# Gate and up products of the feed-forward stages as two by two blocks with seven half-size products

## The chip, the core and the metric

The kernel runs on one core of a Trainium2 chip. The metric is device time in microseconds (us) of one execution of the whole program. The engines that matter are TensorE (PE for its matmuls, PEld for its loads of stationary operands), VectorE (DVE), ScalarE (ACT), GpSimd (POOL) and SyncE (SP), whose queue issues nearly all DMAs.

## The reference, cut to what matters

Two layers of a token mixer and a SwiGLU feed-forward stage over 512 latent and 256 context tokens of width 1024, all float32. Layer 0 carries all 768 tokens; layer 1 computes its feed-forward stage on the 512 latent tokens alone. The change lies in the first product of this stage:

```python
FF_HIDDEN = 2816
def swiglu(h, w_i, w_o):
    g, u = jnp.split(h @ w_i, 2, axis=-1)      # (T,1024) @ (1024, 2*2816)
    return (jax.nn.silu(g) * u) @ w_o
...
xl = xl + ml[5] * rms_norm(swiglu(adaln(xl, g[2], ml[3], ml[4]), w_ffn_in[l], w_ffn_out[l]), g[3])
```

`ml` are per-layer modulation vectors, `silu(c) @ w_mod + b_mod`.

## The kernel before, in words

**Numbers.** A float32 product is made of three float32r matmuls (`mm3`): each operand x is kept as a rounded part hi and a rest lo = x - hi, and hi*hi + hi*lo + lo*hi are summed in PSUM. ACT writes hi, DVE writes lo (one subtraction with two inputs in SBUF). The weights come from DRAM in pieces of 128x1024 into three raw tiles on the chip (`NR = 3`), are split into one of five weight slots (`NW = 5`, `pump`), and the raw tile is then free for the next DMA. Pieces are loaded in one fixed order, `build_seq`. Weights are in reg7r, raw tiles and small things in reg8f; the residual stream X0 is reg6f; the two big regions at A0 (reg0, reg1) and B0 (reg2, reg3) swap roles between layers.

**Feed-forward stage (`ffn`).** The 22 units of 128 hidden columns are taken in groups of 4, 4, 4, 4, 2, 4. For each unit the gate piece and the up piece (128x1024 each: eight blocks of 128 along the inner dimension) are the stationary operands. In layer 0 the tokens stream in two parts of 512 and 256 columns, in layer 1 in one part of 512. So a unit is 2 pieces x 8 blocks x 3 = 48 matmuls for each part. After it, ACT takes the silu of the gate out of PSUM, DVE multiplies it with the up product out of PSUM, and hi and lo of the result are written. After each group the second weight matrix is applied: for each tile of 128 tokens and each half of 512 output columns 3 matmuls per unit of the group (the "w_o stretch" below), and DVE adds the sum to an accumulator in SBUF.

**Modulation vectors on DVE (`gemv_v`).** 56 raw pieces of `w_mod` (one modulation of layer 0, six of layer 1) are interleaved with the weights of layer 0's stage. Each is used by DVE as multiply-adds of 512 columns with two SBUF inputs (four for each of the first 24 pieces, two for each of the other 32); a piece holds one of the three raw tiles until then. PE transposes the results.

**Order.** All instructions are emitted by one program on the host. `Clock` keeps a modelled time for each engine and buffer; `drive` advances the main line (PE's products) and steps side lanes when their modelled due time has come. On the chip every engine runs its own list in order and waits on semaphores. In `Clock` the engines run side by side and never slow each other.

Of the kernel before, what the change touches and what calls it, by code (L numbers as in the profile page):

```python
# [13 lines left out]
ALU = mybir.AluOpType  # L14
# [136 lines left out]
class Builder:  # L151
    def __init__(self, tc, ctx, ins, out):
# [7 lines left out]
        cuts = [A0, A0 + 6144, B0, B0 + 6144, C0, VB, X0, W0, RAW0, self.L.end]  # L160
        self.reg = [[a, b, None, None] for a, b in zip(cuts, cuts[1:])]
        for i, k in enumerate('rrfffffrf'):
            self.mode(i, k)
        self.M = gp.tile([128, 7, 128], U8, name="M")
# [6 lines left out]
        self.narrow = False  # L171
# [20 lines left out]
    def V(self, off, *dims, p0=0, np_=128):  # L192
        a, b, t = self.find(off)
        t0 = t[:, off - a:off - a + 1]
        ps = t0.ap[0][0]
        return bass.AP(t0.tensor, t0.offset + p0 * ps, [[ps, np_]] + [list(d) for d in dims])
# [26 lines left out]
    def mm(self, out, lhsT, rhs, start=True, stop=True):  # L223
        n, m = self.cols(rhs), self.cols(lhsT)
        if rhs.dtype == F32R:
            t = max(0.417 * n, 105)
# [9 lines left out]
        self.nc.tensor.matmul(out, lhsT, rhs, start=start, stop=stop)  # L236

    def mm3(self, out, lh, ll, rh, rl, start, stop):
        r = self.r
        self.mm(out, r(lh), r(rh), start, False)  # L240
        self.mm(out, r(lh), r(rl), False, False)
        self.mm(out, r(ll), r(rh), False, stop)
# [119 lines left out]
    groups = [4, 4, 4, 4, 2, 4]  # L362

    def build_seq(self):
# [15 lines left out]
        for l in range(DEPTH):  # L380
# [23 lines left out]
            for gi, g in enumerate(self.groups):  # L404
                for i in range(2 * f, 2 * (f + g)):
                    w(I['wfi'][l, i])
                    if l == 0 and i > 3 and spread:
                        raw(spread.pop(0), 'g')
                for i in range(f, f + g):
                    w(I['wfo'][l, i])  # L410
                if l == 0:
# [3 lines left out]
        self.seq, ns = [], 0  # L415
        for a, k in seq:
            self.seq.append([a, k, ns, None])
            ns += k == 'w'
# [5 lines left out]

    def pump(self, upto=-1):
        seq, go = self.seq, True
        while go:
            go = False
            if self.n_dma < len(seq) and self.slots:
                it = seq[self.n_dma]  # L430
                it[3] = RAW0 + self.slots.pop(0) * 1024
                self.dma(self.S(it[3], 1024), it[0])
                self.n_dma += 1
                go = True
            while self.n_proc < self.n_dma and seq[self.n_proc][1] != 'w':
                self.n_proc += 1
            if (self.n_proc < self.n_dma and seq[self.n_proc][2] < self.n_freed + NW
                    and (self.n_proc <= upto or self.ck.written(self.S(seq[self.n_proc][3], 1024)) <= self.now + 200)):
                it = seq[self.n_proc]
                w = W0 + (it[2] % NW) * 2048  # L440
                rw = self.S(it[3], 1024)
                if self.n_proc >= self.n_hi:
                    self.act(self.r(self.S(w, 1024)), rw)
                if self.sides[2] and self.nbk == 2 and self.ck.t['po'] + 1200 < self.ck.t['dv']:

                    self.pool(self.r(self.S(w + 1024, 1024)), rw, self.S(w, 1024), ALU.subtract, 2360)
                else:
                    self.tt(self.r(self.S(w + 1024, 1024)), rw, self.S(w, 1024), ALU.subtract)
                self.slots.append((it[3] - RAW0) // 1024)
                self.n_proc += 1  # L450
                go = True

    def get(self):

        while self.seq[self.n_w][1] != 'w':
            self.n_w += 1
        k = self.n_w
        self.n_w += 1
        while k >= self.n_proc:
            self.pump(k)  # L460
            if k >= self.n_proc:
                self.more(force=True)
        assert k < self.n_proc, "stuck"
        return W0 + (self.seq[k][2] % NW) * 2048
# [6 lines left out]
    def get_raw(self, tag='g'):  # L471
# [5 lines left out]
        return self.seq[k][3]  # L477
# [5 lines left out]
    def extra_time(self):  # L483
# [7 lines left out]
        return max(self.ck.written(self.S(self.seq[k][3], 1024)), busy) if k < self.n_dma else None  # L491
# [199 lines left out]
    def proj_t(self, H, tiles, npc, n, cb, ok=None):  # L691
        ws = []
        per = 8 // npc
        for i, t in enumerate(tiles):
            if ok:
                yield lambda: ok(t)
                yield self.ck.written(self.V(H + t * 128, (T, 16), (1, 128)))
# [220 lines left out]
    def attention(self):  # L918
# [100 lines left out]
        def restack():  # L1019
            for hh in range(2):  # L1020
                if hh not in restacked and issued > last[hh] and self.n_prep == 4:
# [3 lines left out]
                    if len(restacked) == 2:  # L1025
                        self.mode(5, 'f')
# [38 lines left out]
    def mixer(self):  # L1065
# [11 lines left out]
        self.mode(0 if l else 2, 'f')  # L1077
# [42 lines left out]
        self.mode(0 if RB == A0 else 2, 'r')  # L1120
        self.mode(5, 'r')
# [110 lines left out]
    def wout(self):  # L1232
# [79 lines left out]
    def wout_norm(self, t, junk):  # L1312
# [4 lines left out]
        self.scaled(t, y)  # L1317
        self.sides[1].append(self.wout_ada(t, y))
# [9 lines left out]
    def ffn(self):  # L1328
# [3 lines left out]
        TS, G5 = A + 6144, A + 9216  # L1332
# [3 lines left out]
        self.mode(1 if A == A0 else 3, 'f')  # L1336

        def unit(wg, wu, slot, parts, free=0):
            bs = {}
            for w in (wg, wu):  # L1340
                for o, n in parts:
                    b = self.bank()
                    bs[w, o] = self.B(b, n)
                    for kc in range(8):
                        self.mm3(bs[w, o], self.S(w + kc * 128, 128), self.S(w + 1024 + kc * 128, 128),
                                 self.S(H2 + kc * T + o, n), self.S(H2 + (8 + kc) * T + o, n), kc == 0, kc == 7)
                        if kc == 7 and w == wu:
                            k = slot % 2
                            s, fu = self.S(TS + k * 1536 + o, n), self.S(TS + k * 1536 + 768 + o, n)
# [347 lines left out]
```

## Time and profile before

| what | value |
|---|---|
| median of 3 runs | 1883.36 us (1878.64 to 1889.82) |
| profiled execution, its own time | 1883.15 us |
| its span in the trace | 1881.0 us, mean granted TensorE clock 0.991 |
| PE busy in the span | 1812.2 us (96%), 11140 matmuls |
| DVE busy | 1040.1 us (55%) |
| ACT busy | 684.0 us (36%) |
| POOL busy | 208.1 us (11%) |

Layer 0's feed-forward stage runs from about 500 to 1110 us after the start of the span, layer 1's from about 1500 us to the end. The 0.00 of the windows below is the start of the span. A row of a windows view has the window, its length, and busy time and number of instructions of PE, PEld, DVE, ACT and POOL, then the granted clock, the DMA share and GB/s. A row of a timeline has start, duration from first start to last end, engine, line, operation, operands and count. A matmul's duration is longer than the distance to the next one, because matmuls overlap; the distance between starts is what a stream of them costs. The same holds, to a smaller degree, for DVE.

### The profile page before, as it was taken

The numbers are of one execution on the slowest core, as the hardware profiler recorded it, in microseconds if no ns is written. First come the engines' busy times: TensorE is split into PE (matmuls) and PEld (weight loads), VectorE is DVE, ScalarE is ACT, GpSimd is POOL, SyncE is SP. The second block draws the span as 40 slices with busy tenths as digits, with TensorE's granted clock in tenths as the row PEclk, the third lists the DMA queues.
The fourth block names the chain that finished last, engine by engine and source line by source line (L and its number), as shares of the span: only waits on it lengthen the run. The fifth ranks groups of instructions, "written<-read, shape, count | busy, mean of one in ns | idle before, by whom it ended". The sixth has DMA issues, their size and how long they took to land.

```text
span 1881.0 us, 27410 instructions
## 1 busy us (share of the span) xinstructions
PE 1812.2 (96%) x11140; PEld 1507.5 (80%) x11140; DVE 1040.1 (55%) x1781; ACT 684.0 (36%) x1374; POOL 208.1 (11%) x287
## 2 busy tenths in 40 slices
PE   6999999997999999999999999999998989999998
PEld 3888886676789888888888878888776788888886
DVE  3478853566475666555455374887476542433444
ACT  4533431357473221212212264333266543222222
POOL 0000003234220000000000040000434100000002
PEclk9999999998999999999999999999999999999999
DMA  9211118442123433434343212111431223243221
GB/s 343 68 57 35 35 53 202 143 83 62 52 106 99 148 124 112 149 120 144 110 144 107 68 45 72 52 46 57 90 79 33 69 88 101 70 121 101 90 90 56
DMA packets 52782, 179.88 MB, mean 96 GB/s; under 512 B 6960, under 2 KB 7856, under 8 KB 52656
## 3 DMA queue, kind: packets, MB, share of 16 engines
q1 hardware_dynamic: 48816, 169.48, 28.3%
q0 software_dynamic: 3840, 8.65, 3.3%
q8 instruction: 87, 1.43, 0.3%
q14 instruction: 39, 0.32, 0.1%
HBM read 167.36 MB, written 2.10 MB: 90 GB/s over the span
## 4 chain that ended last, share of the span: by engine, by line
PE 85%; DVE 5%; ACT 5%; DMA 2%; issue 1%; POOL 1%; SPq 0%; DVEq 0%; POOLq 0%; ACTq 0%
PE P L236 82%; PE P L246 3%; ACT reg1f L257 1%; ACT reg3f L257 1%; DVE reg8f L959 1%; ACT reg7r L257 1%; DVE reg7r L264 1%; ACT reg8f L257 1%; DMA reg4f<-in_wmod 0%; DMA reg8f<-in_wmod 0%; DMA reg0r<-reg5r 0%; DVE reg4f L264 0%; DMA reg8f<-in_wout 0%; ACT reg0r L257 0%; DVE reg8f L276 0%
## 5 line engine op out<-in xcount | busy, mean ns | idle before, releaser
L236 PE MATMUL P<-reg2r,reg7r 128*128 128x256 f32 (+1 forms) x1920 | 481.0, 338 | 0.2 <-ACT reg8f L257 0.2
L236 PE MATMUL P<-reg0r,reg7r 128*128 128x512 f32 (+1 forms) x1344 | 380.3, 363 | 3.9 <-ACT reg0r L257 3.9
L264 DVE TENSOR_TENSOR reg7r<-reg8f,reg7r 128x1024 fp32r<-128x1024 f32 x200 | 243.1, 1225 | 232.7 <-ACT reg7r L257 231.1
L236 PEld LDWEIGHTS P<-reg2r,reg7r 128*128 128x128 f32 x1920 | 330.2, 190 | 39.1 <-issue 0.7
L257 ACT ACTIVATE reg7r<-reg8f 128x1024 fp32r<-128x1024 f32 x204 | 212.8, 1053 | 369.0 <-issue 150.8
L236 PE MATMUL P<-reg7r,reg0r 128*128 128x512 f32 (+1 forms) x1272 | 328.5, 389 | 8.1 <-ACT reg0r L257 6.1
L236 PE MATMUL P<-reg3r,reg7r 128*128 128x512 f32 (+1 forms) x960 | 321.9, 335 | 0.4 <-DVE reg3r L264 0.4
L236 PEld LDWEIGHTS P<-reg0r,reg7r 128*128 128x128 f32 x1344 | 243.1, 191 | 52.5 <-issue 8.4
L236 PEld LDWEIGHTS P<-reg7r,reg0r 128*128 128x128 f32 x1272 | 233.2, 190 | 58.0 <-ACT reg0r L257 7.1
L236 PE MATMUL P<-reg1r,reg7r 128*128 128x512 f32 (+1 forms) x672 | 241.3, 359 | 0.6 <-DVE reg1r L264 0.6
L236 PE MATMUL P<-reg7r,reg2r 128*128 128x512 f32 (+1 forms) x912 | 231.4, 382 | 5.6 <-DVE reg3r L276 1.9
L236 PEld LDWEIGHTS P<-reg7r,reg2r 128*128 128x128 f32 x912 | 165.7, 188 | 39.4 <-ACT reg2r L257 2.3
L236 PEld LDWEIGHTS P<-reg3r,reg7r 128*128 128x128 f32 x960 | 182.4, 190 | 18.5 <-issue 0.7
L236 PEld LDWEIGHTS P<-reg1r,reg7r 128*128 128x128 f32 x672 | 128.3, 191 | 18.7 <-DVE reg1r L264 1.1
L276 DVE SCALAR_TENSOR_TENSOR reg8f<-reg8f 128x512 f32<-128x512 f32 (+3 forms) x154 | 87.6, 569 | 10.6 <-DMA reg8f<-in_wmod 7.7
L236 PE MATMUL P<-reg7r,reg1r 128*128 128x512 f32 (+1 forms) x240 | 90.6, 378 | 0.1
L959 DVE TENSOR_REDUCE reg8f<-P 128x1 f32<-128x768 f32 (+1 forms) x80 | 67.5, 846 | 30.3 <-PE P L236 30.1
L284 POOL TENSOR_TENSOR reg8f<-reg8f 128x1 f32<-128x1 f32 (+2 forms) x102 | 60.2, 592 | 182.5 <-ACT reg5f L257 98.5
L257 ACT ACTIVATE reg3f<-P,reg8f 128x768 f32<-128x768 f32 (+3 forms) x96 | 52.6, 569 | 59.2 <-DVE reg8f L959 46.8
L257 ACT ACTIVATE reg0r<-reg1f 128x256 fp32r<-128x256 f32 (+1 forms) x46 | 23.5, 511 | 135.4 <-DVE reg1f L264 135.4
L236 PE MATMUL P<-reg7r,reg3r 128*128 128x512 f32 (+1 forms) x192 | 70.0, 364 | 0.0
L257 ACT ACTIVATE reg3f<-P 128x512 f32<-128x512 f32 (+2 forms) x106 | 45.1, 442 | 65.5 <-PE P L246 34.7
(218 smaller groups left out, 2012.0 us busy)
## 6 DMA issues: line engine op xcount, KB each, us to landing
reg8f<-in_wfi SPq DMA_DIRECT2D x88, 512.0 KB, 3.6
reg8f<-in_wmod SPq DMA_DIRECT2D x80, 512.0 KB, 3.7
reg8f<-in_win SPq DMA_DIRECT2D x56, 512.0 KB, 3.6
reg8f<-in_wfo SPq DMA_DIRECT2D x44, 512.0 KB, 3.6
reg8f<-in_wout SPq DMA_DIRECT2D x16, 512.0 KB, 4.2
reg6f<-in_xin SPq DMA_DIRECT2D x12, 512.0 KB, 6.3
reg2r<-reg5r POOLq DMA_DIRECT2D x24, 192.0 KB, 6.0
reg2f<-in_wmod SPq DMA_DIRECT2D x8, 512.0 KB, 6.4
```

The costliest lines, as they stand in the source:

```text
L236: self.nc.tensor.matmul(out, lhsT, rhs, start=start, stop=stop)
L246: self.nc.tensor.transpose(out, in_, self.S(self.L.ident, 128))
L257: self.nc.scalar.activation(out=out, in_=in_, func=func, **kw)
L264: self.nc.vector.tensor_tensor(out=out, in0=a, in1=b, op=op)
L276: self.nc.vector.scalar_tensor_tensor(out=out, in0=a, scalar=s, in1=b, op0=op0, op1=op1)
L284: self.nc.gpsimd.tensor_tensor(out=out, in0=a, in1=b, op=op)
L959: self.nc.vector.tensor_reduce(out=sm(i, 2 + m), in_=x, axis=AX.X, op=ALU.min)
```

## The change

Groups 1 to 5 of both layers (18 of 22 units each) compute gate and up together as a 2x2 block product with seven half-size products (Winograd's form of Strassen's algorithm). Rows of blocks: gate and up; inner halves: blocks 0 to 3 and 4 to 7; token halves B.1 and B.2 of 384 columns in layer 0 and 256 in layer 1. With A11, A12 the gate's and A21, A22 the up's inner halves:

- of the weights, for each unit: S3 = A11 - A21, S2 = A22 - S3, S1 = A21 + A22, S4 = A12 - S2 (`sums`, `split_s2`, `split_s4`: four additions of 512 columns); A11, S2, [S3 A12], S4, [S1 A22] are split into hi and lo, in four weight slots in place of two;
- of the tokens, once per layer: T1 = B12 - B11, T2 = B22 - T1, T3 = B22 - B12, T4 = B21 - T2 (`tblocks`, two side lanes). T1 and T3 go into X0 in layer 0 and into unused columns in layer 1, T4 overwrites B12 and so is made only after group 0;
- for each unit (`pair`) the products A11*B11, S2*T2, S1*T1, A12*B21, S3*T3, S4*B22, A22*T4 of 4 blocks x 3 matmuls, some added onto an older one's bank in PSUM; the rest of the sums is done on DVE and ACT, one of them by `sum2`.

`sum2` puts an addition on POOL or DVE by their modelled free times. Layer 0's residual X0 is written to DRAM tiles `xs` in `wout_norm` and read back before group 5's w_o stretch. The 56 pieces of `w_mod` come from group 1 on, no longer from group 0. The w_o stretch visits the tiles of the second token half first.

```diff
+    def sum2(self, out, a, b, op):
+        n = self.cols(out)
+        if max(self.ck.t['po'], self.now) + 2.4 * n < max(self.ck.t['dv'], self.now) + 1.4 * n + 700:
+            self.pool(out, a, b, op, 2.36 * n)
+        else:
+            self.tt(out, a, b, op)
...
+            elif k == 'b':
+                ab = [first, i]
+                self.task(0, self.split_a11, ab[:1])
+                self.task(None, self.sums, ab)
+                self.task(None, self.split_s2, ab)
+                self.task(0, self.split, ab[:1])
+                self.task(0, self.split_s4, ab[:1], ab[:1])
+                self.task(0, self.split, ab[1:], ab[1:])
...
+    def sums(self, w, a, b):
+        a, b, tmp = self.raw(a), self.raw(b), self.S(self.L.u, 512)
+        a11, a21, a22 = self.S(a, 512), self.S(b, 512), self.S(b + 512, 512)
...
+        self.sum2(a11, a11, a21, ALU.subtract)
+        self.sum2(tmp, a22, a11, ALU.subtract)
+        self.sum2(a21, a21, a22, ALU.add)
...
+        self.halves(w, 512, tmp, 512, lambda: self.sum2(tmp, self.S(self.raw(a) + 512, 512), tmp, ALU.subtract))
...
+            def diff(p, q):
+                self.sum2(t1, p[0], q[0], ALU.subtract)
+                self.sum2(t1, t1, p[1], ALU.add)
+                self.sum2(t1, t1, q[1], ALU.subtract)
...
+            for kc in range(4):
+                diff(at(B21, kc), at(T2, kc))
+                yield self.ck.t['dv']
+                put(T4, kc, t1)
...
+            def late():
+                self.sum2(p5, p5, u3, ALU.add)
...
+                self.act(q6, q6, AF.Silu)
...
+                self.tt(p5, p5, q6, ALU.mult)
...
+                yield from put(p5, hw)
...
+            yield from prod(z, B11, ba, True)
+            self.act(c1, self.B(ba, hw))
+            yield from prod(z + 512, T2, bb, True)
+            self.done()
...
+            self.tt(q6, c1, self.B(bb, hw), ALU.add)
+            y, w4, x = self.get(), self.get(), self.get()
+            bc = self.bank()
+            yield from prod(x, T1, bc, True)
...
+            self.act(p5, self.B(bc, hw))
+            yield from prod(y + 512, B21, ba, False)
+            self.act(s1, self.B(ba, hw), AF.Silu)
+            yield from prod(y, T3, bb, False)
+            self.done()
+            self.tt(u3, c1, self.B(bb, hw), ALU.add)
+            yield from prod(w4, B22, bc, False)
+            self.done()
+            self.tt(q6, q6, self.B(bc, hw), ALU.add)
+            self.sides[2].append(late())
+            yield lambda: self.n_t == 4
+            bd = self.bank()
+            yield from prod(x + 512, T4, bd, True)
+            self.done()
+            self.tt(u3, u3, self.B(bd, hw), ALU.add)
+            self.tt(u3, u3, s1, ALU.mult)
+            self.sides[0].append(put(u3, 0))
...
+        if self.spill:
+            self.dma(self.xs[t], self.S(X0 + t * 1024, 1024))
...
+                if fast and l == 0:
+                    self.mode(8, 'f')
+                    for t in tiles:
+                        self.dma(self.S(X0 + t * 1024, 1024), self.xs[t])
```

More of the change, by code (lines that the diff above doesn't have):

```diff
@@ L193, in V @@
         a, b, t = self.find(off)
+        assert off + sum((n - 1) * st for st, n in dims) < b
         t0 = t[:, off - a:off - a + 1]
@@ new lines, in flush, with task @@
+    def flush(self, upto):
+        while self.lows and (self.lows[0][3] <= upto or self.ck.written(self.lows[0][0]) <= self.now + 150):
+            _, low, frees, _ = self.lows.pop(0)
+            low()
+            for k in frees:
+                self.slots.append((self.raw(k) - RAW0) // 1024)
+    def task(self, new, fn, needs, frees=()):
+        if new is not None:
+            self.ends.append(0)
+        self.tasks.append((len(self.ends) - 1, fn, needs, frees))
+        self.ends[-1] = len(self.tasks)
@@ L425, in pump, with split_s4 @@
+    def split_s4(self, w, a):
+        tmp = self.S(self.L.u, 512)
+        yield self.ck.written(tmp) if not any(lo[3] == self.n_proc - 1 for lo in self.lows) else 1e12
+        self.halves(w, 0, tmp, 512)
     def pump(self, upto=-1):
@@ L437, in pump @@
[L437 to L451, printed above, removed]
+            if self.n_proc < len(self.tasks):
+                slot, fn, needs, frees = self.tasks[self.n_proc]
+                if needs[-1] < self.n_dma and slot < self.n_freed + NW:
+                    g = fn(W0 + (slot % NW) * 2048, *needs)
+                    if next(g) <= self.now + 200 or self.n_proc < upto:
+                        if self.n_proc < upto:
+                            self.flush(self.n_proc)
+                        next(g, None)
+                        if frees:
+                            self.lows[-1][2] = frees
+                        self.n_proc += 1
+                        go = True
@@ L490, in extra_time @@
         k = self.rq['g'][0]
-        return max(self.ck.written(self.S(self.seq[k][3], 1024)), busy) if k < self.n_dma else None
+        return max(self.ck.written(self.S(self.raw(k), 1024)), busy) if k < self.n_dma else None
     def extra_due(self):
@@ new lines, in ffn @@
+            for t in order:
+                y, bs = YA[t], {}
+                if t == order[0]:
+                    todo = [(nh, i) for nh in range(2) for i in range(g - 1)] + [(nh, g - 1) for nh in range(2)]
+                elif t == order[-1]:
+                    todo = [(nh, i) for i in range(g) for nh in range(2)]
+                else:
+                    todo = [(nh, i) for nh in range(2) for i in range(g)]
+                for m, (nh, i) in enumerate(todo):
+                    if nh not in bs:
+                        bs[nh] = self.bank()
+                        yield self.ck.free(bs[nh])
+                    if t == order[0] and nh == 0 and fast and gi:
+                        yield lambda: put_.get(i) == 2
+                    if i == len(ws):
+                        ws.append(self.get())
+                    self.mm3(self.B(bs[nh]), self.S(A + i * 1536 + t * 128, 128), self.S(A + i * 1536 + 768 + t * 128, 128),
+                             self.S(ws[i] + nh * 512, 512), self.S(ws[i] + 1024 + nh * 512, 512), i == 0, i == g - 1)
+                    if t == order[-1] and nh:
+                        self.done()
+                    if i == g - 1:
+                        evict(t, nh, bs[nh])
+                    if m % 2:
+                        yield
@@ L1429, in ffn @@
                     self.more()
+        while self.extra:
+            self.more(force=True)
     def ffn_fin(self, t, yo, G5, TS, l, H):
```

256 lines of the change are left out of this document (185 added, 71 removed).

## The prediction, made before the change was run

> **What bounds the kernel now.** I read first the page's totals and chain, then the windows view of the feed-forward stages, then the distances in the timeline.
>
> ```profile
> PE 1812.2 (96%) x11140; PEld 1507.5 (80%) x11140; DVE 1040.1 (55%) x1781; ACT 684.0 (36%) x1374; POOL 208.1 (11%) x287
> PE 85%; DVE 5%; ACT 5%; DMA 2%; issue 1%; POOL 1%; SPq 0%; DVEq 0%; POOLq 0%; ACTq 0%
> ```
>
> TensorE sets the end, over the whole span. The stages that the change touches, layer 0 first (group 0's units 0 and 1 and their neighbours, then gate/up of group 1, its w_o stretch, gate/up of groups 2, 3 and 5), then a gate/up and a w_o stretch of layer 1:
>
> ```profile
> 584.50:615.90 31.40, 31.40 (x188) 27.94 (x187) 22.47 (x30) 9.33 (x13) 0.00 (x0) 1.00 0.56 185
> 615.90:649.90 34.00, 34.00 (x158) 28.19 (x157) 23.07 (x39) 9.72 (x15) 0.00 (x0) 1.00 0.38 120
> 649.90:718.50 68.60, 68.60 (x402) 60.71 (x401) 41.19 (x59) 16.84 (x26) 0.00 (x0) 1.00 0.44 140
> 718.50:752.00 33.50, 33.50 (x153) 27.77 (x153) 24.29 (x39) 3.12 (x4) 0.00 (x0) 1.00 0.29 93
> 752.00:820.10 68.10, 68.10 (x397) 60.23 (x397) 34.65 (x49) 16.28 (x25) 0.00 (x0) 1.00 0.42 140
> 853.20:920.80 67.60, 67.60 (x394) 59.88 (x394) 32.31 (x44) 16.16 (x25) 0.00 (x0) 1.00 0.45 140
> 1006.40:1073.50 67.10, 67.10 (x390) 59.42 (x389) 22.60 (x30) 15.43 (x24) 0.00 (x0) 1.00 0.28 87
> 1576.70:1620.20 43.50, 43.50 (x194) 36.03 (x193) 16.68 (x17) 13.57 (x18) 0.00 (x0) 1.00 0.44 133
> 1620.20:1642.00 21.80, 21.80 (x98) 17.96 (x97) 8.09 (x11) 3.43 (x4) 0.00 (x0) 1.00 0.08 25
> ```
>
> PE is busy for the whole of every row at a full clock; nothing else holds it. VectorE is the next engine: 41.19 of 68.60 us in group 1's gate/up stretch. POOL does nothing there.
>
> **TensorE's saving.** Two pairs of rows of layer 0's timeline, at widths 512 and 256:
>
> ```profile
> 650.38 0.62 PE L236 MATMUL P<-reg2r,reg7r 128*128 128x512 f32 x2
> ...
> 654.46 0.62 PE L236 MATMUL P<-reg2r,reg7r 128*128 128x512 f32 x2
> ...
> 655.60 0.40 PE L236 MATMUL P<-reg2r,reg7r 128*128 128x256 f32 x2
> ...
> 657.76 0.40 PE L236 MATMUL P<-reg2r,reg7r 128*128 128x256 f32 x2
> ```
>
> Each pair spans 18 matmuls: 4.08 / 18 = 0.2267 us at 512 columns, 2.16 / 18 = 0.120 at 256. A width of 384 does not occur in such a stream; it lies between, and halfway is 0.1733, which I take (the ends 0.120 and 0.2267 are the bounds; a load that held it up would have held the 256 too). Layer 0: a unit is 48 x (0.2267 + 0.120) = 16.64 us now and 7 x 12 x 0.1733 = 14.56 after: 2.08 less, 37.4 over 18 units. Layer 1: 48 x 0.2267 = 10.88 now (43.50 / 4 says the same), 84 x 0.120 = 10.08 after: 0.80 less, 14.4 over 18 units. Together **-51.8 us**. This many matmuls go: 18 x (96 - 84) in layer 0; 18 x (84 - 48) come in layer 1.
>
> **What VectorE gets.** Durations of one, and how close two follow:
>
> ```profile
> L264 DVE TENSOR_TENSOR reg7r<-reg8f,reg7r 128x1024 fp32r<-128x1024 f32 x200 | 243.1, 1225 | 232.7 <-ACT reg7r L257 231.1 <-PE P L236 0.5
> L276 DVE SCALAR_TENSOR_TENSOR reg8f<-reg8f 128x512 f32<-128x512 f32 x98 | 73.4, 749 | 8.6 <-DMA reg8f<-in_wmod 7.7
> ...
> 649.23 2.36 DVE L264 TENSOR_TENSOR reg7r<-reg8f,reg7r 128x1024 fp32r<-128x1024 f32 x2 [1.93 <-ACT reg7r L257]
> ...
> 654.22 0.75 DVE L276 SCALAR_TENSOR_TENSOR reg8f<-reg8f 128x512 f32<-128x512 f32 x1 [0.91 <-DMA reg8f<-in_wmod]
> 654.89 0.75 DVE L276 SCALAR_TENSOR_TENSOR reg1f<-reg8f,reg1f 128x512 f32<-128x512 f32 x1
> ...
> 133.33 1.02 DVE L264 TENSOR_TENSOR reg3f<-reg3f 128x384 f32<-128x384 f32 x2
> ```
>
> A second 1024 subtraction ends 2.36 - 1.225 = 1.135 us after the first; a 384 one costs 0.47 in the same way (two in 1.02, each 0.55). The line through both gives 0.60 at 512 and 0.34 at 256. A unit of layer 0 costs DVE now two weight subtractions (2.27) and a multiply and a subtraction for 512 and for 256 columns (2 x 0.94): 4.15 us. After: weight subtractions of 3 x 512 and 2 x 1024 columns, 4.07; four weight sums, 2.40; nine operations of 384 columns on the results, 4.23: **10.7 us of 14.56**. In layer 1: 3.47 now, 4.07 + 2.40 + 9 x 0.34 = **9.5 of 10.08** after. The split's ACT part grows from 2 to 3.5 copies of 1024; ACT is at 16.84 of 68.60 us and is not late.
>
> Layer 0 also has the modulation pieces. Group 1's row less its units, 41.19 - 16.6 = 24.6 us, is mostly these. They now start a group later, so that the 24.6 stay with group 1, group 2 gets some of its heaviest pieces (24 rather than the 34.65 - 16.6 = 18.1 of its row), group 3 what group 2 had, the last groups some 16. Demand in the gate/up stretches of groups 1, 2, 3, 5: 42.8 + 24.6 = 67.4, 67, 61 and 59 us. PE needs 4 x 14.56 and about 2 us of transposes (68.60 less 4 x 16.64): 60. So VectorE asks for 7 us too much in each of groups 1 and 2 and is level in the rest. The w_o stretches have room (9 of 33.5 us idle in the fullest), but pieces and weights can be made ahead by the free ones of five slots and three raw tiles alone, a few us of work; I take **+10 us** for layer 0, between 0 (all of it made ahead) and 14 + some stalls, 20.
>
> **T blocks.** T1 to T3 are 44 operations of 384 columns (20.7 us; 15 in layer 1). They run under group 0's last two units and its w_o stretch, where the modulation work is taken away: hidden by those 66 us, in which DVE had 20 us idle before that. Without that cover they would cost their 21 and 15 us. T4 can't be hidden so: 16 operations, 7.5 us (layer 0) and 5.4 us (layer 1), start with group 1 and must be done before the first pair's seventh product, 6 x 2.08 = 12.5 and 6 x 1.44 = 8.6 us later. DVE has that pair's own work too, and in layer 0 a quarter of 24.6: 7.5 + 10.7 + 6.1 = 24 us, and 5.4 + 9.5 = 15. Part of the pair's work isn't due before its end, and PE's wait lets the rest catch up; I take **+5 us in each layer** (0 to 11 and 0 to 6).
>
> **In order, nearly full.** In layer 1, DVE at 9.5 of 10.08 us must serve both PE's next weights and the PSUM banks that products 4, 5 and 6 add onto; a weight subtraction waits behind a result that waits for PE. I take 0.3 us for each of 18 pairs, **+5** (0 to 10).
>
> **POOL takes sums.** The rule in `sum2` chooses POOL when its modelled free time is at most 0.19 us later than DVE's (512 columns). That is often, with DVE this full.
>
> ```profile
> L284 POOL TENSOR_TENSOR reg1f<-reg1f,reg8f 128x256 f32<-128x256 f32 x4 | 2.9, 733 | 0.3
> ...
> 1097.82 1.29 POOL L284 TENSOR_TENSOR reg4f<-reg4f,reg1f 128x512 f32<-128x512 f32 x1 [0.81 <-ACT reg1f L257]
> ...
> 1096.84 0.68 DVE L264 TENSOR_TENSOR reg4f<-reg4f,P 128x512 f32<-128x512 f32 x1
> 1098.53 1.12 DVE L264 TENSOR_TENSOR reg4f<-reg4f,reg1f 128x512 f32<-128x512 f32 x1 [1.01 <-ACT reg1f L257]
> ```
>
> A sum on POOL is 1.29 us against 0.60. And the two don't run side by side: the last row, with two operands in SBUF, starts inside POOL's 1.29 and takes 1.12 where its twin from PSUM took 0.68; it ends 0.54 us after POOL's end at 1099.11. So a 512 sum moved to POOL may take 1.29 of time that DVE's two-SBUF operations can't use, 0.69 more than it frees; only operations with a PSUM operand (four in a pair, 1.9 or 1.4 us) can run beside it. With two of the four weight sums and the last sum moved (0.73 against 0.34 in layer 1), that is 2 x 0.69 + 0.39 = 1.8 us less up to 1.4 of overlap, so about 0.5 us a pair. If DVE were the bound in layer 1's 18 pairs and in the 8 of groups 1 and 2 it would be 13; since it is only near the bound in most of them I take **+8** (0 to the price of the second rival).
>
> The Trainium skill states this as a rule (SBUF — State Buffer, "Who interferes with whom"): a DVE instruction with two SBUF inputs and a GpSimd instruction that reads SBUF hold a shared port in turn, and the second blocks fully. The 1.12 against 0.68 agrees. Taken in full it gives the second rival's sum; without it the term would be nothing.
>
> **DMA.** X0's way out and back is 12 x 512 KB on SP's queue.
>
> ```profile
> reg8f<-in_wfi SPq DMA_DIRECT2D x88, 512.0 KB, 3.6
> reg6f<-in_xin SPq DMA_DIRECT2D x12, 512.0 KB, 6.3
> ```
>
> The way out waits on SP for values already there, ahead of weights that land in 3.6 us. The way back is issued after the last pair, waits for its T3 product and holds SP for the next layer's weights, which are not wanted before the 33 us w_o stretch is over; the first row of X0 is wanted after that stretch's first tile, some 5.5 us, against 6.3. I take 0, at most 3.
>
> **The sum.** -51.8 + 10 + 10 + 5 + 8 = -18.8. The profiled execution took 1883.15 us (span 1881.0 and 2.15 around it), within 0.2 us of the median of 1883.36. Forecast **1864 us**.
>
> **Rivals.**
> 1. *All is hidden.* The added work is made ahead in the w_o stretches and PE stays at 100%. For it: DVE idles 9 to 14 us in every w_o stretch, and the demand over a whole group of layer 0 (67.4 + 24.3 against 60 + 33.5) still fits. Against: the ring of weight slots is short. Only the T4 waits stay, at half: -52 + 5: 1836.
> 2. *The shared path of DVE and POOL becomes the bound (slower).* All four weight sums and the last one go to POOL. A pair of layer 1 then needs 4.07 + 4 x 0.34 on DVE's two-SBUF side and 4 x 1.29 + 0.73 on POOL: 11.3 us against 10.08, +1.2 x 18 = 22. In layer 0: 4.07 + 4 x 0.47 + 4 x 1.29 + 1.0 = 12.1, and the modulation work of 6.1, 4.5 and 4 us: above PE's 15 a unit by 3.2 in groups 1 and 2, 1.6 in 3, 1 in 4 and 5: 26 + 6 + 6 = 38. T4 on POOL: +13. Together +73 - 52: 1904. It decides from about three of the five sums on POOL in layer 1; the planner's clock, which lets both engines run freely, speaks for it, and the four PSUM operations a pair against.
> 3. *VectorE alone eats the saving* (the change doesn't do what it says): PE waits for weights in every pair of layer 0 up to the old pace, 2.08 x 18 given back, and layer 1 keeps its 14 less 10 for T4 and order: 1880. For it: 10.7 + 6.1 = 16.8 us a unit in groups 1 and 2, above the old 16.64. Against: groups 3 to 5.
>
> **Chances.** Forecast 0.48, rival 1 0.15, rival 2 0.20, rival 3 0.17. The forecast's own range, with its 33 us of losses at 0.6 to 1.5 of what I took, is 1851 to 1881. 0.5% is 9.4 us, about what a measurement of this kernel tells from nothing: faster means under 1874, slower above 1893. Faster: rival 1 and 0.44 of the forecast's 0.48, 0.59. Slower: rival 2's, with a little of it falling short, 0.19. Same: the rest, 0.22. The range that should hold it, 1834 to 1899, cuts off the upper part of rival 2 and a little below rival 1.
>
> **What would show it.** 11140 + 432 = 11572 matmuls; a distance of 0.173 at 384 columns. In gate/up of groups 1 and 2, PE idle before loads of reg weights with DVE as releaser, 3 to 10 us a stretch; in groups 3 and 5 stretches of 60 to 62 us; in layer 1 stretches of 41 to 43 us after a first one of 46 or more, with a wait of PE for T4 (written in B12's place) in the first pair of each layer. DVE busy near 1300 us, and its two-SBUF subtractions longer than 1.225 and 0.69 wherever POOL runs beside them. Wrong: if PE is still at 100% in groups 1 and 2 (rival 1), if POOL has over 150 us more and layer 1's stretches are above 43.5 (rival 2), or if 384 columns cost more than 0.18.

## The result and the profile after

The changed kernel takes **1948.1 us** (median of 4 runs, 1942.43 to 1950.17) against 1884.11 of the kernel before: a ratio of **1.0335, 95% interval 1.0296 to 1.0373**. It is 64 us slower; the forecast was 1864 and the range ended at 1899.

In the changed kernel's names the weights are reg9r, raw tiles reg10f, X0 with T1 and T3 reg8; the helpers stand three lines lower (matmul L239, ACT L260, two-input subtraction and addition L267, multiply-add L279, POOL L287). From its page, the totals, the chain and one group:

```profile
PE 1801.7 (93%) x11572; PEld 1547.6 (80%) x11572; DVE 1287.1 (66%) x2163; ACT 797.3 (41%) x1622; POOL 470.8 (24%) x496
...
PE 61%; DVE 19%; DMA 6%; ACT 6%; POOL 4%; issue 4%; SPq 0%; DVEq 0%; POOLq 0%; ACTq 0%
...
L287 POOL TENSOR_TENSOR reg10f<-reg10f 128x512 f32<-128x512 f32 (+3 forms) x210 | 217.3, 1036 | 594.2 <-DMA reg10f<-in_wfi 219.8
```

The matmuls are the 11572 foreseen. The span is 1945.2 us, 64.2 longer: losses of two kinds, less the 51.8 us that the matmuls save. TensorE's idle time (span less busy) is 143.5 us against 68.8: **+74.7**. Its busy time fell by 10.5 us where the matmul saving was 51.8: **+41.3**. The second kind is, for the most part, the clock: its mean over the span is 0.971 against 0.991. Where it falls it stands at 0.50 (below), so 2 x 0.029 x 1945 = 113 us ran at half speed instead of 34. Half of the 79 more is 39.5, an upper bound, since in some of that time TensorE was waiting anyway. Laid over its busy time in the two traces, the half speed grows from 25 to 89 us, which costs 32 of the 41.3; the rest was not taken apart.

The windows of gate/up of layer 0 (groups 1 and 2) and of layer 1 (groups 1, 2, 3 and 5):

```profile
641.20:725.50 84.30, 68.81 (x354) 65.00 (x353) 70.87 (x101) 27.90 (x46) 24.67 (x18) 0.90 0.37 118
761.30:847.60 86.30, 70.19 (x354) 66.86 (x353) 71.08 (x100) 29.07 (x45) 21.02 (x14) 0.88 0.38 120
...
1617.30:1668.10 50.80, 43.90 (x338) 42.72 (x337) 38.42 (x58) 25.25 (x47) 20.69 (x18) 0.93 0.30 101
1693.90:1739.10 45.20, 42.27 (x338) 41.87 (x337) 35.33 (x52) 22.69 (x40) 15.87 (x13) 0.96 0.35 115
1763.30:1807.10 43.80, 40.91 (x338) 40.50 (x337) 35.74 (x52) 22.62 (x41) 15.88 (x13) 1.00 0.36 120
1868.20:1914.30 46.10, 43.17 (x346) 42.77 (x345) 35.39 (x52) 23.88 (x43) 15.88 (x13) 0.96 0.28 92
```

Layer 0's first two stretches took 68.60 and 68.10 before and should now need 60; layer 1's took 43.50. Each row has idle TensorE, a clock below 1.00 or both, and POOL at work where it did nothing. Who was waited for, in the first of these windows and then in all of layer 1 from group 1 on:

```profile
PE P L239 <- DVE reg9r L267: 4.9, 3, 2.8
PE P L239 <- ACT reg9r L260: 4.7, 2, 3.9
PE P L239 <- ACT reg3r L260: 3.5, 2, 2.9
PE P L239 <- DVE reg4r L267: 2.4, 1, 2.4
...
PE P L239 <- DVE reg5f L267: 11.1, 8, 1.7
PE P L239 <- DVE reg3r L267: 6.8, 4, 2.3
```

The columns are total, times and longest. In layer 0 the waits are for weights (reg9r) and for T4 in B12's place (reg3r, reg4r); in layer 1 VectorE's results (reg5f) come too late to free a PSUM bank.

The timeline of the same kernel in layer 1, VectorE first, then GpSimd, shows the two together:

```profile
1772.71 0.41 DVE L267 TENSOR_TENSOR reg5f<-reg5f,P 128x256 f32<-128x256 f32 x1
...
1779.99 0.41 DVE L267 TENSOR_TENSOR reg5f<-reg5f,P 128x256 f32<-128x256 f32 x1
...
1781.70 2.00 DVE L267 TENSOR_TENSOR reg9r<-reg10f,reg9r 128x1024 fp32r<-128x1024 f32 x1 [0.26 <-ACT reg9r L260]
...
1799.62 1.22 DVE L267 TENSOR_TENSOR reg9r<-reg10f,reg9r 128x1024 fp32r<-128x1024 f32 x1
...
1772.27 1.12 POOL L287 TENSOR_TENSOR reg5f<-reg5f 128x256 f32<-128x256 f32 x1 [1.49 <-DVE reg5f L267]
...
1781.53 1.09 POOL L287 TENSOR_TENSOR reg10f<-reg10f 128x512 f32<-128x512 f32 x1 [2.08 <-DVE reg9r L267]
```

POOL's sum lasts from 1781.53 to 1782.62. The subtraction that starts within it takes 2.00 us, the one with POOL idle 1.22: 0.78 of the 0.92 us of overlap is lost. An operation with a PSUM operand takes 0.41 us within a GpSimd sum (1772.71) as with GpSimd idle (1779.99). The weight sums of the whole kernel, from its groups by shape:

```profile
L287 POOL TENSOR_TENSOR reg10f<-reg10f 128x512 f32<-128x512 f32 x108 | 156.4, 1448 | 418.9 <-DMA reg10f<-in_wfi 219.8 <-DVE reg9r L267 162.8 <-DVE reg10f L267 24.1
...
L267 DVE TENSOR_TENSOR reg10f<-reg10f 128x512 f32<-128x512 f32 x44 | 32.4, 735 | 43.9 <-POOL reg10f L287 43.6
```

The mean on POOL is 1.45 us where the sum at 1781.53, which began before the subtraction, took 1.09.

And the clock, in windows of 3 us behind the T4 waits of layer 0 (2.39 us until 658.37, 2.88 until 661.87), and behind a single wait of 2.12 us that ends at 904.20:

```profile
658.00:661.00 3.00, 0.62 (x2) 0.30 (x2) 1.90 (x4) 0.52 (x1) 2.17 (x2) 0.67 0.00 0
661.00:664.00 3.00, 2.13 (x6) 1.83 (x7) 2.88 (x6) 2.46 (x4) 0.40 (x1) 0.50 0.00 0
664.00:667.00 3.00, 3.00 (x14) 3.00 (x13) 3.00 (x4) 1.76 (x3) 1.14 (x1) 0.69 0.12 23
667.00:670.00 3.00, 2.50 (x15) 2.18 (x14) 2.97 (x5) 0.84 (x2) 0.00 (x0) 1.00 0.84 289
...
904.80:908.20 3.40, 3.40 (x13) 3.40 (x12) 2.76 (x5) 0.61 (x2) 0.00 (x0) 0.50 0.53 155
```

The two waits are followed by a clock of 0.50 to 0.69 for over 6 us, while TensorE is needed again. The single one is followed by 3.40 us at 0.50, with TensorE busy throughout.

### The profile page after: what moved, and what is told of

Same layout as the page of the kernel before. It is cut to its first block, busy times and chain, and to the rows that moved or that the text cites. A ratio compares the mean times of both kernels' runs of the same rounds, so it can differ in the third digit from the quotient of the medians.

```text
span 1945.2 us, 29322 instructions
## 1 busy us (share of the span) xinstructions
PE 1801.7 (93%) x11572; PEld 1547.6 (80%) x11572; DVE 1287.1 (66%) x2163; ACT 797.3 (41%) x1622; POOL 470.8 (24%) x496
## 4 chain that ended last, share of the span: by engine, by line
PE 61%; DVE 19%; DMA 6%; ACT 6%; POOL 4%; issue 4%; SPq 0%; DVEq 0%; POOLq 0%; ACTq 0%
PE P L239 58%; DVE reg9r L267 5%; DMA reg10f<-in_wfi 4%; PE P L249 3%; POOL reg10f L287 3%; DVE reg10f L279 2%; DVE reg2f L267 2%; DVE reg10f L1043 1%; ACT reg9r L260 1%; DVE reg10f L267 1%; DVE reg5f L267 1%; DMA reg10f<-in_wmod 1%; POOL reg5f L287 1%; DVE reg2f L279 1%; ACT reg4f L260 1%
## 5 line engine op out<-in xcount | busy, mean ns | idle before, releaser
L260 ACT ACTIVATE reg9r<-reg10f 128x1024 fp32r<-128x1024 f32 (+1 forms) x312 | 277.0, 906 | 343.1 <-PE P L239 111.0
L267 DVE TENSOR_TENSOR reg9r<-reg10f,reg9r 128x1024 fp32r<-128x1024 f32 (+1 forms) x305 | 336.8, 1116 | 95.1 <-ACT reg9r L260 93.6
L239 PE MATMUL P<-reg0r,reg9r 128*128 128x256 f32 (+1 forms) x1632 | 367.9, 315 | 19.5 <-DVE reg5f L267 11.1
L287 POOL TENSOR_TENSOR reg10f<-reg10f 128x512 f32<-128x512 f32 (+3 forms) x210 | 217.3, 1036 | 594.2 <-DMA reg10f<-in_wfi 219.8
L239 PE MATMUL P<-reg3r,reg9r 128*128 128x384 f32 (+2 forms) x1344 | 356.2, 342 | 3.6 <-ACT reg3r L260 3.5
L239 PE MATMUL P<-reg9r,reg0r 128*128 128x512 f32 (+1 forms) x1272 | 328.3, 389 | 10.3 <-ACT reg0r L260 7.4
L239 PEld LDWEIGHTS P<-reg0r,reg9r 128*128 128x128 f32 x1632 | 274.6, 194 | 46.8 <-DVE reg5f L267 12.7
L239 PEld LDWEIGHTS P<-reg9r,reg0r 128*128 128x128 f32 x1272 | 234.4, 190 | 59.3 <-ACT reg0r L260 8.4
L239 PEld LDWEIGHTS P<-reg3r,reg9r 128*128 128x128 f32 x1344 | 241.1, 192 | 20.8 <-ACT reg3r L260 4.2
L239 PE MATMUL P<-reg9r,reg3r 128*128 128x512 f32 (+1 forms) x912 | 236.7, 387 | 15.3 <-DVE reg3r L267 6.8
L239 PEld LDWEIGHTS P<-reg9r,reg3r 128*128 128x128 f32 x912 | 168.3, 191 | 51.2 <-DVE reg3r L267 8.9
L239 PE MATMUL P<-reg1r,reg9r 128*128 128x256 f32 (+2 forms) x624 | 172.1, 327 | 11.3 <-ACT reg9r L260 6.5
L239 PE MATMUL P<-reg4r,reg9r 128*128 128x256 f32 (+2 forms) x552 | 142.7, 317 | 2.4 <-DVE reg4r L267 2.4
L239 PEld LDWEIGHTS P<-reg1r,reg9r 128*128 128x128 f32 x624 | 119.3, 196 | 18.4 <-ACT reg9r L260 7.4
L239 PE MATMUL P<-reg2r,reg9r 128*128 128x256 f32 (+1 forms) x408 | 126.8, 311 | 0.0
L239 PE MATMUL P<-reg8r,reg9r 128*128 128x384 f32 x432 | 94.8, 365 | 25.6 <-DVE reg9r L267 19.9
L239 PE MATMUL P<-reg5r,reg9r 128*128 128x384 f32 (+2 forms) x336 | 113.4, 338 | 0.0
L239 PEld LDWEIGHTS P<-reg8r,reg9r 128*128 128x128 f32 x432 | 81.3, 205 | 31.3 <-DVE reg9r L267 23.9
L279 DVE SCALAR_TENSOR_TENSOR reg10f<-reg10f 128x512 f32<-128x512 f32 (+3 forms) x154 | 96.0, 624 | 5.6 <-DMA reg10f<-in_wmod 2.9
L260 ACT ACTIVATE reg5f<-P 128x256 f32<-128x256 f32 (+2 forms) x132 | 51.9, 405 | 116.6 <-PE P L239 54.4
L260 ACT ACTIVATE reg2f<-P 128x384 f32<-128x384 f32 (+3 forms) x118 | 53.6, 465 | 111.8 <-PE P L239 71.0
```

Source lines behind the costliest of these rows:

```text
L260: self.nc.scalar.activation(out=out, in_=in_, func=func, **kw)
L267: self.nc.vector.tensor_tensor(out=out, in0=a, in1=b, op=op)
L279: self.nc.vector.scalar_tensor_tensor(out=out, in0=a, scalar=s, in1=b, op0=op0, op1=op1)
L287: self.nc.gpsimd.tensor_tensor(out=out, in0=a, in1=b, op=op)
```

## The experiments

Theory: GpSimd's sums slow VectorE (the second rival), and under that VectorE's own load in layer 0, the late T4 and a half clock after each wait add up. Rivals: the raw tiles or DMAs hold the weights; the edits outside the products cost it; the products themselves are no cheaper. A difference below is to the kernel before in the same session (+64.0 for the changed kernel).

**Sums on VectorE alone (e1_no_pool).** In `sum2`:

```diff
-        if max(self.ck.t['po'], self.now) + 2.4 * n < max(self.ck.t['dv'], self.now) + 1.4 * n + 700:
+        if False:
```

> The changed kernel, but every sum of sum2 goes to VectorE; POOL gets none. Theory A (the path that VectorE and POOL share): a weight subtraction of 1024 columns that overlaps a POOL sum takes 1.57 us in layer 0 and 1.79 in layer 1 in place of 1.22, a multiply-add 1.28 in place of 0.75; without POOL all are back at 1.22 and 0.75, layer 1's gate/up stretches come down from 43.8 to 50.8 us to 41 to 44, and the time falls by 25 to 50 us, to about 1900 to 1925. Theory B (VectorE's own load is the bound, POOL only relieved it): some 90 POOL sums of 0.6 us each more on VectorE, the time rises by 10 to 50 us, to 1960 or more. Theory C (raw tiles, slots and DMA hold PE, not engine time): within 5 us of 1948.

1915.31 us, ratio 1.0164 (1.0139 to 1.0189): +32.1, so the sums on GpSimd cost **31.9 us**. Its windows, layer 0's groups 1 and 2 and layer 1's groups 1 and 2:

```profile
640.40:719.90 79.50, 66.42 (x354) 62.78 (x353) 72.38 (x121) 26.86 (x45) 0.00 (x0) 0.94 0.36 115
755.80:837.40 81.60, 68.25 (x354) 63.93 (x353) 72.99 (x115) 28.35 (x45) 0.00 (x0) 0.94 0.41 132
1606.00:1654.20 48.20, 43.71 (x338) 42.45 (x337) 42.28 (x79) 25.88 (x47) 0.00 (x0) 0.93 0.34 108
1677.30:1717.90 40.60, 40.60 (x338) 40.38 (x337) 36.73 (x64) 23.00 (x41) 0.00 (x0) 1.00 0.40 127
```

VectorE does more operations (64 instead of 52 in layer 1's group 2) in hardly more time (36.73 against 35.33), and TensorE has no wait left there. Layer 1's first stretch, where T4 is made, stays at 48.20 and so above the expected 41 to 44. Layer 0 remains far above 60.

**None and one layer alone (e2_none, e3_layer1, e4_layer0).** The layers with seven products are chosen by one line. The other edits stay, but three go with the layer: the later start of the pieces and X0's way through DRAM are in e4 alone, the new order of the w_o tiles is in e3 and e4:

```diff
-    fast = (0, 1)
+    fast = (9,)      # e2; (1,) in e3; (0,) in e4
```

> The changed kernel with both layers' stages in the old eight-product form (fast empty): what stays are the new order of loading and splitting weights, the moved token and gate buffers, the new matmul cost in the planner and the new order within the w_o stretch. Theories A, B and C: 1884 within 8 us, as before. Theory D (these other edits cost time of their own): above 1895.

> Seven products in layer 1 only; layer 0 as before, its modulation work spread as before, X0 stays on the chip. If the two layers' losses add: layer 1's stretches were 1.6 + 22.6 + 1 us longer in the changed kernel than before, so 1905 to 1912. Theory A expects DVE's 1024 subtractions beside POOL at 1.8 us as in the changed kernel. If the loss needs the modulation work (theory B, layer 0 alone): 1884 or less.

> Seven products in layer 0 only. If the two layers' losses add: 1884 + 45 + 3 - 9 = 1923, within 6 us. Theory A and B expect the same here; the stretches of groups 1 and 2 stay at 84 to 87 us.

1889.23 us, ratio 1.0022 (1.0010 to 1.0034): +6.1. 1909.28, 1.0132 (1.0113 to 1.0151): +26.1. 1929.03, 1.0238 (1.0209 to 1.0267): +45.9. The two layers add up: 26.1 + 45.9 less the 6.1 that both contain is 65.9, against 64.0. Both lose, and the other edits are a small part. In e2 TensorE is idle for 7.6 us between 500 and 1160, mostly at the end of layer 0, against 2.9 in the kernel before; what makes it wait was not tried.

**T4 during group 0 (e5_t4_early).** e1, and T4 is made from the end of group 0's gate and up products on, not with group 1's start:

```diff
-            while self.n_t < 3:
+            while self.n_t < 2 or not self.g0:
...
+            self.g0 = True          # behind the gate and up units of a group
```

> The kernel without POOL sums, and T4 is made as soon as group 0's gate and up products are done, under its w_o stretch, in both layers (B12 isn't read later than that). If PE's waits in the first pair of each layer are the wait for T4: layer 1's first stretch goes from 48.3 to about 41 us, layer 0's from 79.6 to about 72, and the time from 1915 to 1895 to 1903. If these waits are VectorE's order and load at a group's start: within 4 us of 1915.

1903.59, 1.0092 (1.0077 to 1.0108): +18.1, 14.0 less than e1 and just above the expected 1895 to 1903. Layer 0's groups 1 and 2, then layer 1's group 1:

```profile
639.00:708.80 69.80, 63.28 (x354) 61.18 (x353) 64.55 (x106) 25.10 (x42) 0.00 (x0) 0.98 0.42 133
744.30:826.30 82.00, 68.26 (x354) 63.83 (x353) 73.05 (x115) 28.35 (x45) 0.00 (x0) 0.94 0.41 130
...
1592.00:1639.20 47.20, 43.25 (x338) 42.16 (x337) 41.25 (x76) 25.50 (x47) 0.00 (x0) 0.96 0.34 111
```

Group 1 of layer 0 gained 9.7 us, that of layer 1 only 1.0, not the 7 that were expected: there T4 still came late.

**Modulation pieces from group 0 on, as before the change (e6_mods_g0).** e5, and

```diff
-                    if l == 0 and i > (7 if self.fast[0] == 0 else 3):
-                        for _ in range(min(len(spread), 1 + (i in (13, 17, 21, 25, 29, 33, 37)) * (self.fast[0] == 0))):
+                    if l == 0 and i > 3:
+                        for _ in range(min(len(spread), 1)):
```

> The kernel before this one in the list, with the modulation pieces spread from group 0 on, as before the change (eight of 56 leave groups 1 to 5). If VectorE's load in layer 0 is what holds PE (41 us of multiply-adds less what fits into group 0's idle 46 us): 10 to 20 us below the run with T4 early, near 1880 to 1888. If the raw tiles that the pieces occupy hold PE (theory C): they occupy them still, no change within 5 us.

1904.95, 1.0102 (1.0087 to 1.0117): no gain over e5. By the number this is the rival's forecast, the raw tiles. The waits from 600 to 672.6 us, which hold group 0's w_o stretch, and three windows, that stretch and the gate/up of groups 1 and 2:

```profile
PE P L239 <- ACT reg9r L260: 21.7, 4, 13.3
```

```profile
607.20:672.60 65.40, 43.40 (x186) 33.61 (x185) 45.46 (x77) 15.97 (x28) 0.00 (x0) 0.79 0.28 89
672.60:748.40 75.80, 65.81 (x354) 62.58 (x353) 67.56 (x108) 28.81 (x47) 0.00 (x0) 0.95 0.41 128
782.20:850.10 67.90, 62.41 (x350) 61.01 (x349) 59.33 (x95) 25.37 (x42) 0.00 (x0) 0.97 0.43 135
```

The w_o weights come 13.3 us late, and the clock falls to a mean of 0.79. The timeline shows the order, VectorE first, then SyncE's queue:

```profile
616.20 0.75 DVE L279 SCALAR_TENSOR_TENSOR reg10f<-reg10f 128x512 f32<-128x512 f32 x1
...
618.96 17.88 SPq L299 DMA_DIRECT2D reg10f<-in_wfo  x4
```

VectorE makes token sums up to 616.20, then works off a piece (four multiply-adds, until 618.94), and only then are the w_o weights loaded: the piece held its raw tile while VectorE was late. Group 1's gate/up starts 33.6 us later than in e5 and takes 6 us more; what e6 gains comes after it, where group 2 takes 67.90 in place of 82.00.

**Narrow modulation pieces (e7_narrow_mods).** e5, with each multiply-add of `gemv_v` on 32 of its 512 columns; the rest of the modulation products is left out. Pieces, DMAs and their order stay.

```diff
+                            o, w = self.S(acc[c], 32), self.S(rw + q * 512, 32)
```

> The run with T4 early, but the modulation multiply-adds of layer 0's stage work on 32 of 512 columns (the rest of these products is left out, so the modulation vectors are wrong): same pieces, same DMAs, same raw tiles, about 0.2 us in place of 0.75 for each of 140 instructions. Theory B' (VectorE's load in layer 0): demand in group 1's gate/up falls from 67 to about 47 us against PE's 60, the stretches of groups 1 and 2 fall to 60 to 64 us, the time to 1855 to 1870. Theory C (raw tiles and DMA): within 8 us of the run with T4 early.

1863.81, 0.9884 (0.9869 to 0.9899): -21.7, **39.8 us** less than e5. The time lies where theory B' expected it, the stretches somewhat above its 60 to 64. Layer 0's groups 1 and 2:

```profile
638.80:705.30 66.50, 62.76 (x354) 61.42 (x353) 52.06 (x107) 26.96 (x43) 0.00 (x0) 0.97 0.47 152
738.90:804.50 65.60, 61.18 (x354) 59.64 (x353) 52.44 (x110) 25.53 (x41) 0.00 (x0) 1.00 0.50 160
```

The same bytes move, at 160 GB/s where e5 has 130 in group 2, so the DMAs were not the hold; VectorE's time on the pieces was, together with the raw tiles that they keep for that time; no run parts these two.

**Waits put into the kernel before (e9_stalls).** Before each unit of layer 1, ACT copies 256 columns of the PSUM bank just finished three times and then writes part of a weight slot again, so that TensorE must wait:

```diff
+                if l:
+                    for _ in range(3):
+                        self.act(self.S(TS, 256), self.B(self.cur, 256))
+                    self.act(self.r(self.S(wg, 128)), self.S(wg, 128))
```

> The kernel before the change, with one added wait of PE ahead of each of 20 units of layer 1: three ACT copies of 256 columns out of the bank just filled, and one of ACT's copies over the first 128 weight columns, which the next matmul reads; some 1.5 to 2 us of PE idle each. If a wait costs its own length and no more: 1884 + 30 to 40, as the sum of PE's idle says. If PE's idle also lets its granted clock fall to a half for 3.4 us at a time, as it seems after the waits in the changed kernel: a further 1.7 us for each fall, up to 34 more.

2008.93, 1.0661 (1.0643 to 1.0680). From 1519 us to the end, the kernel before, and then this one, with three windows around a wait of 3.76 us that ends at 1611.36:

```profile
1519.00:1881.00 362.00, 352.59 (x1592) 292.69 (x1592) 138.94 (x159) 97.03 (x132) 11.75 (x16) 0.99 0.29 90
```

```profile
1519.00:2005.40 486.40, 394.74 (x1600) 317.33 (x1598) 140.94 (x165) 124.56 (x218) 11.75 (x16) 0.90 0.22 67
...
1600.00:1603.00 3.00, 3.00 (x15) 2.49 (x14) 0.00 (x0) 0.98 (x2) 0.00 (x0) 1.00 0.25 97
...
1609.00:1612.00 3.00, 0.64 (x3) 0.54 (x4) 1.92 (x2) 2.25 (x6) 0.00 (x0) 0.98 0.00 0
1612.00:1615.00 3.00, 3.00 (x9) 2.33 (x8) 0.00 (x0) 0.00 (x0) 0.00 (x0) 0.50 0.54 175
```

TensorE's idle time there grows from 9.4 to 91.7 us, by 82.3: the 20 waits are some 4 us each, twice as long as meant, so that the time misses the expected sum. Its busy time grows by 42.1, of which some 2 us are 8 matmuls more in the window: each wait cost **about 2 us on top of its length**. At a clock of 0.50, 9 matmuls fit in 3 us instead of 15. The Trainium skill (TensorE: Matmul & The Clock Gate, "HAM oscillation — how this bites in real kernels") tells of this oscillation and gives about 3.4 us as the shortest idle gap that brings it. The waits of e9, most of them 3.76 us or more, agree with that, but in the changed kernel 2.39 and 2.88 us, one right after the other, were enough, and so was the single wait of 2.12 us.

**Pieces dealt out evenly (e10_spread).** e5, T1 to T4 begun as soon as their tokens are there, one piece beside each unit (in group 5 beside each weight piece), the others behind the w_o groups:

```diff
-                    if l == 0 and i > (7 if self.fast[0] == 0 else 3):
-                        for _ in range(min(len(spread), 1 + (i in (13, 17, 21, 25, 29, 33, 37)) * (self.fast[0] == 0))):
+                    if l == 0 and i > 7 and (i % 2 or gi == 5):
+                        for _ in range(min(len(spread), 1)):
...
-                    for i in range(min(g, len(spread))):
+                    for i in range(min(g + 3, len(spread))):
```

> The kernel of e5 (no weight sums on GpSimd, T4 made in group 0), with the token sums T1 to T4 begun as soon as their tokens are there, and the modulation pieces of layer 0 dealt out differently: one beside each unit of the gate and up products instead of several, the others behind the w_o groups. Theory (VectorE's load in the gate and up stretches of layer 0's groups 1 to 3 is what holds TensorE there): those stretches fall from about 70-80 to 61-66 us, layer 1's first stretch to 41-44, and the time to 1868-1885 us, not under the 1863.8 of the run with narrow modulation pieces. Rival (the pieces' raw tiles hold up the w_o weights, as in e6): the w_o stretch of group 0 grows by 10 to 30 us and the time is 1895 us or more.

1888.39, 1.0014 (1.0003 to 1.0024): +2.3, 15.8 less than e5 but outside the 1868 to 1885 that was expected. Gate/up of groups 1, 2, 3 and 5, then layer 1's first:

```profile
640.00:702.40 62.40, 60.58 (x345) 58.88 (x346) 57.90 (x91) 28.99 (x45) 0.00 (x0) 1.00 0.42 130
738.70:811.00 72.30, 64.31 (x345) 62.35 (x346) 62.40 (x99) 28.46 (x45) 0.00 (x0) 0.93 0.36 115
846.50:910.20 63.70, 60.91 (x341) 60.13 (x342) 54.58 (x88) 28.47 (x44) 0.00 (x0) 0.97 0.40 130
996.80:1075.60 78.80, 66.71 (x361) 63.60 (x362) 61.62 (x96) 30.85 (x49) 0.00 (x0) 0.92 0.43 136
1587.90:1628.50 40.60, 40.60 (x338) 40.29 (x337) 35.91 (x62) 23.73 (x43) 0.00 (x0) 1.00 0.42 130
```

Groups 1 and 3 came down as the theory has it. Group 2 stayed at 72.30, above the expected 61 to 66 (82.00 in e5), and group 5 rose from 74.00 to 78.80, where TensorE waits for the rounded parts (hi) of the weights, written by ACT:

```profile
PE P L239 <- ACT reg9r L260: 9.0, 3, 5.1
```

Dealing out differently moves some of the load; it does not take it away. The rival's longer w_o stretch did not come: group 1 starts at 640.00 us, at 639.00 in e5. The earlier T sums end layer 1's late T4: 40.60 against 47.20.

**Part of the modulations on TensorE (e11_pe_mods).** e5 with the early T sums, and the first 24 of the 56 pieces multiplied by TensorE (`gemv`):

```diff
-                self.extra = self.gemv_v(self.ffn_mods, self.get_raw, self.done_raw, 5, (L.km, A + 11776))
+                def mods():
+                    yield from self.gemv(self.ffn_mods[:3], self.get_raw, self.done_raw, 5, lambda: L.km)
+                    yield from self.gemv_v(self.ffn_mods[3:], self.get_raw, self.done_raw, 5, (L.km, A + 11776))
+                self.extra = mods()
```

> The kernel of e5 with earlier token sums, and the first three of the seven modulations of layer 0 (24 weight pieces) multiplied on TensorE, the others on VectorE as before. Theory (VectorE's load is the hold): the time is that of narrow modulation pieces, 1863.8, plus 13 us of matmuls (24 pieces x 2 x 0.27) plus what is left on VectorE: 1875-1890 us, groups 1 and 2 of layer 0 at 61-66 us for a gate and up stretch. Rival (raw tiles and their DMAs hold, not VectorE's work): no gain over e5's 1903.6, or a loss of about the 13 us of matmuls.

**1876.47, 0.9943 (0.9926 to 0.9960): 9.6 us faster than the kernel before**, the best complete kernel of this study. The time lies in the expected 1875 to 1890; the stretches of 61 to 66 us do not hold:

```profile
640.40:711.70 71.30, 71.30 (x385) 60.11 (x383) 42.67 (x69) 27.97 (x45) 0.00 (x0) 1.00 0.47 151
752.60:822.00 69.40, 68.94 (x378) 60.03 (x377) 41.60 (x69) 26.19 (x42) 0.00 (x0) 1.00 0.41 135
```

TensorE is busy for all or nearly all of both, at a full clock. They are longer than expected because the modulation matmuls run in them, 385 and 378 matmuls in all where e5 has 354.

**e11's two layers apart (e12_l1_lanes, e13_l0_pe_mods).** Layer 1 alone, with the early T sums; layer 0 alone, with the 24 pieces on TensorE:

```diff
-    fast = (0, 1)
+    fast = (1,)      # e12; (0,) in e13
```

> Only layer 1 with seven products, weight sums on VectorE alone, token sums T1 to T4 begun as soon as their tokens are there; layer 0 with eight products and its modulation pieces as before. Theory (layer 1 has no other fault than GpSimd's sums and a late T4): gate and up stretches of 40.6 to 41 us for four units instead of 43.5, all of them, the first too; w_o stretches of 23.2 against 21.8 stay. So about -12 for 18 units, +5 for the w_o stretches and a wait of 2.9, +6 for the other edits: 1880 to 1890 us against some 1885 of the kernel before. Rival (the seven products pay in layer 1 as a whole): 1872 to 1878, and then layer 0 earns nothing in the kernel with the modulations on TensorE.

> Only layer 0 with seven products, weight sums on VectorE alone, early token sums, 24 of the 56 modulation pieces multiplied on TensorE; layer 1 with eight products as before. Theory (VectorE's load was layer 0's fault, and with it moved layer 0 keeps part of its 37.4): 1876.5 plus what layer 1 earned in that kernel, which the run beside this one shows; if the two parts add, its difference from the kernel before and that of the layer 1 kernel come to the -9.6 measured, less the +6 of the other edits counted twice. Rival (layer 0 loses still): 1890 us or more.

1880.76, 0.9984 (0.9974 to 0.9993): -2.9. 1886.44, 1.0013 (1.0001 to 1.0025): +2.8. Less the +6.1 of the other edits, layer 1 earns 9.0 us and layer 0 3.3, of the 14.4 and 37.4 that their products save by the prediction. With the 6.1 taken once, -6.2 would be e11's difference, against -9.6 measured in another session. Neither rival's time came (1872 to 1878; 1890 or more). So even without GpSimd layer 0's saving goes nearly whole to the work that must be done beside it, the modulation matmuls on TensorE included. Which part of that work takes how much was not tried.

## Why the prediction was wrong, step by step

Two terms of the sum failed above all by their size, VectorE's load in layer 0 and GpSimd's sums, and one cost was put at nothing: the slower clock of TensorE after a wait. The terms in turn:

**TensorE's saving: right.** In e11, layer 0's group 4, 12 matmuls of 384 columns lie between the starts of these rows:

```profile
962.64 0.34 PE L239 MATMUL P<-reg3r,reg9r 128*128 128x384 f32 x1
...
964.73 1.55 PE L239 MATMUL P<-reg8r,reg9r 128*128 128x384 f32 x8
```

2.09 / 12 = 0.174 us, where 0.1733 was taken. Layer 1's four units without a wait take 40.60 us, where 40.3 was worked out.

**POOL takes sums: the mechanism was right, its size wrong by four.** +8 was taken, 31.9 measured. Of 144 weight sums 108 went to POOL (VectorE makes 44 additions of this shape, 152 in e1), three of four in a unit and not two. The price of 0.5 us a pair was too small, and so was the discount to the pairs where VectorE was taken for the bound: for all 36 pairs 0.5 would be 18, and 31.9, with the token sums on POOL in it, is 0.9 a pair. The second rival had the time of layer 1 right, in part by luck: 11.3 us a pair, or 45.2 for four; 45.20, 43.80 and 46.10 were measured. But it moved all five sums of a pair, and three weight sums and the last one went. Its own rows then give 4.07 + 0.60 + 4 x 0.34 + 3 x 1.29 + 0.73 = 10.6, or 42.5 for four; waits and the clock (0.96 in two of the three stretches) made the rest. Both signs named for it appeared (POOL 263 us more, layer 1's stretches above 43.5). The Trainium skill's rule (SBUF — State Buffer, "Who interferes with whom") taken in full, as in that rival, would have been nearer than the forecast; 2.00 against 1.22 us agrees with it.

**VectorE's load in layer 0: the view was right, +10 against 39.8.** The demand of 67 us against 60 was seen, and then less than this difference was charged, 10 us for twice 7. In e5, whose group 2 has no T4 in it, VectorE works 73.05 us, 6 more than taken, in a stretch of 82.00. So its own idle time of 9 us adds to the excess, as it would where two engines wait for each other in order, and TensorE's clock falls to 0.94 besides. e7 takes away nearly all of the pieces' work and not the excess alone, but the kernel before did the same work with TensorE busy throughout, so 39.8 is a cost that the change brought. The third rival also named this; it and the second came true together, while each was priced as if the other did not exist.

**T4: +10 against about 20.** 14.0 by e5 and, in layer 1, 47.20 less 40.60 by the early sums. In order, nearly full: +5 for layer 1; its gate/up stretches lose nothing without POOL, but its w_o stretches have waits for the last unit's result, 5.8 us in e11. From 1577 us, the start of layer 1's group 1, to the end its waits are these two rows and no other:

```profile
PE P L239 <- DVE reg3r L267: 2.9, 3, 1.0
PE P L239 <- ACT reg3r L260: 2.9, 1, 2.9
```

**Other edits: 0 against 6.1** (e2); not taken apart. X0's way through DRAM and the new order of the w_o tiles are not in e2, and no run tried them alone; in the changed kernel's profile no engine is seen waiting for X0's return.

**What was missing altogether:** that a wait of TensorE costs more than its length. The sum counted waits alone. Of the 116 us of losses (74.7 + 41.3) the second part lies in TensorE's busy time, and e9 shows waits making such a cost.

As differences the path back from the changed kernel closes: +64.0, less 31.9 (GpSimd), 14.0 (T4) and 39.8 (pieces) leaves -21.7. To the full -51.8 it lacks 30.1: 6.6 of T4 in layer 1, 5.8 and 6.1 as above, and 11.6 that no run took apart (e7's stretches in layer 0 have waits of TensorE left: 66.50 less 62.76 us in the first). These are costs in this order of removal; in another order they would differ.

## What to carry to other kernels

A scheme that trades matmuls for additions is worth what the engine of the additions has left, stage by stage. In layer 1 VectorE was busy for 90% of a stretch (36.73 of 40.60 us in e1) and TensorE did not wait in it; in layer 0, where it was asked for more than TensorE's time, the loss was larger than the excess. There take work off it before, as e11 does. Do not send additions with SBUF operands to GpSimd to relieve VectorE's two-SBUF operations: in these runs they held each other up. Price every new wait of TensorE at its length and, where it is of some 4 us as in e9, some 2 us more for the clock.

## What the runs showed of the hardware that was not expected

- After waits of TensorE of 2.1 to 3.8 us the granted clock stood at 0.50 for 3 us or more: about 2 us extra for each of 20 waits of some 4 us.
- When a GpSimd sum and a two-SBUF operation of VectorE meet, either can be the one that loses. The sum that began first took 1.09 us and the subtraction 2.00 instead of 1.22; the sum at 1772.27, begun while VectorE was at work on two SBUF operands (1772.11, 0.68 us), took 1.12 where one of 256 columns takes 0.73, and the mean of all weight sums on POOL was 1.45.
